# Two-layer macaron transformer block on one core: the last summed weight block of each down projection used at the very end, one gate/up chunk of the first layer by seven products instead of two, second quarter of x turned after the first products

## The chip, the cores and the metric

One core of a Trainium2 chip runs the whole program. The engines have their own in-order instruction streams: TensorE (PE in the profile; its weight loads are PEld), VectorE (DVE), ScalarE (ACT), GpSimd (POOL) and SyncE (SP), which here only issues DMAs. The metric is the device time of one execution in microseconds, median of several.

## The reference, cut to what matters

```python
D_MODEL = 1024; SEQ = 256; DEPTH = 2; D_FF = 2816

def swiglu(x, w_gate, w_up, w_down):
    return (jax.nn.silu(x @ w_gate) * (x @ w_up)) @ w_down

for l in range(DEPTH):
    x = x + 0.5 * swiglu(rms_norm(x, ffa_norm[l]), ffa_w_gate[l], ffa_w_up[l], ffa_w_down[l])
    x = x + hybrid_mixer(rms_norm(x, mix_norm[l]), ...)
    x = x + 0.5 * swiglu(rms_norm(x, ffb_norm[l]), ffb_w_gate[l], ffb_w_up[l], ffb_w_down[l])
return rms_norm(x, final_norm)
```

All arrays are float32. The change touches only the four feed-forward stages (swiglu), which are called A0, B0, A1 and B1 below, after their weights (ffa, ffb) and layer. The mixers (attention and its projections) stand between A and B of a layer.

## The kernel before, in words

**Three matmuls for one product.** float32 operands are split into a high part in fp32r (a rounded copy, `whi` or `xhi`) and the rest (`wlo`, `xlo`). A product is high by high, low by high, high by low: lines 323, 324 and 325, three matmuls of 128x512. A weight block of 1 MB is loaded into a `raw` buffer (five of them), and split in two halves of 128x1024: ACT copies the half to `whi` (line 304), then DVE subtracts to get `wlo` (line 283). There are six pairs of `whi`/`wlo` buffers, so splits run at most three blocks ahead of PE.

**Seven products for eight.** The 256 tokens are two halves t, the 1024 inputs two halves, and gate and up columns of a 512-wide chunk c are two blocks. Gate and up of a chunk are thus a 2x2 by 2x2 block product. It is done directly (in a plan: `g2` and `u2`, 48 matmuls each with both token halves), or as Strassen-Winograd by seven products of 12 matmuls (`11 51 21 31 61 71 41` for chunk 1, the first digit being the product). Five of the seven use sums of blocks. Sums of x are made by DVE (`fnhi`, `fohi` hold their two parts). Sums of weights are made by the DMA queue of POOL: the `raw` buffer of the block before is kept, and once both its halves are split, a DMA with `accum_op=OP.add` adds the next block into it. Products 1, 5, 6, 4 form one such chain in one `raw` buffer, 3 and 7 another, 2 stands alone. A chain keeps its buffer from its first to its last product.

**The down projection.** The same seven products (`1d` to `7d`) do rows 0 to 511 and 1024 to 1535 of the 2816 rows of w_down against chunks 0 and 2 of the hidden values; the other rows are done directly, in blocks of 256 rows (`p2`, `p8`, ..., 24 matmuls each: two token halves by two column halves). The list `DOWN` is the order. Its last `TAIL = 2` blocks, p7 and p10, are done column half by column half and token half by token half, so that each of the four output blocks (t, c) is closed (`close`, line 846: DVE adds it to x) as early as its last product, and the next stage's norm can turn it (four transposes on PE, line 409, then `xhi` on ACT and `xlo` on DVE).

**Order of the work.** A planner (class `Flow`) steps generators by estimated times and writes each engine's stream in that order. Splits are written in the order of the plan's blocks (`units_`), `raw` loads on SP's queue likewise, sums on POOL's queue. `ARRIVE` and `ARRIVE_X` are the planner's times at which the first blocks of weights and the quarters of x arrive; until the planner's time 8, PE is fed warm-up matmuls (`warm`) whenever it has nothing else.

Of the kernel before, what the change touches and what calls it, by code (L numbers as in the profile page):

```python
# [30 lines left out]
TAIL = 2  # L31
# [7 lines left out]
COLD = 5.0  # L39
WARM = 8  # L40
ARRIVE = [4.4, 5.2, 6.7, 7.4], [8.9, 9.6, 11.1, 11.8]
ARRIVE_X = [3.5, 5.9, 8.1, 10.3]
HOP = 0.3
PLANS = ("g0 u0 g2 11 u2 51 21 31 13 61 71 g4 41 53 23 33 u4 63 73 h5 43".split(),) + (
    "g0 u0 11 g2 51 21 31 u2 61 71 13 g4 41 53 23 33 u4 63 73 h5 43".split(),) * 3
DOWN = "1d p2 2d p8 5d p9 3d p3 6d p6 7d 4d p7 p10".split()
AHEAD = 1
AC = 0.1
DV = 0.06
# [85 lines left out]
def hybrid_kernel(ctx, tc, x_in, ffa_norm, ffa_w_gate, ffa_w_up, ffa_w_down, mix_norm, w_in,  # L135
# [14 lines left out]
    fl = Flow()  # L150
# [5 lines left out]
    def bank(tag, bufs):  # L156
        return psum.tile([128, 512], F32, name=tag, tag=tag, bufs=bufs)
# [63 lines left out]
    def order(src, a, b, loads=1, **k):  # L221
        return Unit(Raw(src, a, b, loads), fine=loads > 1, **k)
# [92 lines left out]
    def free_w(u=None):  # L315
        fl.put("w", 0)

    def cols(w, c0, n, kh):
        return w[kh * 512:(kh + 1) * 512, c0:c0 + n].rearrange("(k p) n -> p k n", p=128)
# [8 lines left out]
    def prod(ps, xs, t, k, u, i, sl, first, last):  # L328

        xh, xl = (z[:, k, t * 128:(t + 1) * 128] for z in xs)  # L330
        wh, wl = (z[:, sl] for z in u.part(i))
        prod3(ps, xh, xl, wh, wl, first, last)
# [113 lines left out]
    def ffn_units(wg, wu, wd, plan, first):  # L446

        us = {}  # L450
        chain = {}

        def block(c, m, kh):
            if c == "d":
                r = (0, 2)[kh] * 512
                return wd[r:r + 512, m * 512:(m + 1) * 512].rearrange("(k p) n -> p k n", p=128)
            return cols((wg, wu)[m], c * 512, 512, kh)

        def step(key, c, p, m, kh, end):

            src = block(c, m, kh)
            if key not in chain:
                chain[key] = (Raw(src, 4, 512), None)
                r = chain[key][0]
            else:
                r = Sum(chain[key][0], src, chain[key][1])
            us[p, c] = Unit(r, done=end)
            chain[key] = (chain[key][0], us[p, c])

        for z in plan + DOWN:  # L470
            kind = z[0]
            c = "d" if z[1] == "d" else int(z[1:])
            if kind == "p":
                src = wd[c * 256:(c + 1) * 256].rearrange("(i p) n -> p i n", i=2)
                us["d", c] = order(src, 2, 1024)
            elif kind in "gu":
                m = "gu".index(kind)
                for kh in range(2):
                    us[z, kh] = order(block(c, m, kh), 4, 512, loads=4 if first and z == plan[0] else 1)
            elif kind == "h":  # L480
                for kh in range(2):
                    us[z, kh] = order([cols(wg, 2560, 256, kh), cols(wu, 2560, 256, kh)], 4, 512)
            elif kind in "1564":
                step(("x", c), c, kind, *{"1": (0, 0), "5": (1, 0), "6": (1, 1), "4": (0, 1)}[kind], kind == "4")
            elif kind in "37":
                step(("y", c), c, kind, *{"3": (1, 1), "7": (1, 0)}[kind], z == [q for q in plan + DOWN if q[0] in "37" and q[1:] == z[1:]][-1])
            else:
                step(("z", c), c, kind, 0, 1, True)
        return us

    def ffn(us, nm, nxt, plan, last=False):
# [6 lines left out]
        inner = [i for i, z in enumerate(plan) if z[0] in "1234567"]  # L498
# [96 lines left out]
        def plain(z, tag, first):  # L595
            c, then = int(z[1:]), {"g": gate, "u": up, "h": both}[z[0]]
            ps = {}
            for kh in range(2):
                u = us[z, kh]
                order_ = [(t, i) for t in range(T) for i in range(4)] if first and nm.gi else [(t, i) for i in range(4) for t in range(T)]  # L600
                for t, i in order_:
                    k = kh * 4 + i
                    yield nm.turned[k, t]
                    yield u.when(i)
                    if k == 0:
                        yield fl.get(tag)
                        ps[t] = bank(tag, 4 if tag == "acc" else 2)
                    prod(ps[t], nm.xs, t, k, u, i, slice(0, 512), k == 0, k == KT - 1)
                    if k == KT - 1:
                        fl.spawn(then(c, t, ps[t], tag))  # L610
                    yield
                    if t and i % 2:
                        free_w()
# [86 lines left out]
            fl.spawn(sums(), 1)  # L700


        dforms, dk = {}, {}

        def sums_d():
# [39 lines left out]
        for i, z in enumerate(plan):  # L745
            if i == len(plan) - AHEAD:
                fl.spawn(sums_d(), 1)
            if z[0] in "1234567":
                yield from product(z[0], int(z[1:]))
            else:  # L750
                yield from plain(z, "sb" if inner and i > inner[0] else "acc", i == 0)
        if last:
            yield from last()
        pd = {}
# [22 lines left out]
        def add_x(src, f, t, c):  # L777
            xv = x[:, t, c * 512:(c + 1) * 512]
            nc.vector.scalar_tensor_tensor(xv, src, f, xv, op0=OP.mult, op1=OP.add)
            e = fl.dve(512)  # L780
            event("x", t, c).set(e)
            return e

        def rest_d():
            yield event("D1")
            yield fl.get("p")
            s = md([128, 512], "p", NP)
            nc.scalar.activation(s, dk["1"], AF.Copy)
            e = fl.act(512)
            yield e  # L790
            fl.put("sb", 0, e)
            add_x(s, 0.5, 0, 0)
            yield event("D5")
            yield fl.get("p")
            w = md([128, 512], "p", NP)
            nc.scalar.activation(w, dk["5"], AF.Copy)
            fl.put("sb", 0, fl.act(512))
            yield event("D6")
            nc.vector.tensor_tensor(s, s, dk["6"], OP.subtract)
            e = fl.dve(512)  # L800
            fl.put("sb", 0, e)
            yield e
            nc.vector.tensor_tensor(w, w, s, OP.add)
            yield fl.dve(512)
            add_x(w, -0.5, 0, 1)
            yield event("D7")
            nc.vector.tensor_tensor(w, w, dk["7"], OP.add)
            yield fl.dve(512)
            nc.vector.tensor_tensor(s, s, dk["7"], OP.add)
            e = fl.dve(512)  # L810
            fl.put("sb", 0, e)
            yield e
            fl.put("p", 0, add_x(w, -0.5, 1, 1))
            fl.put("p", 0, add_x(s, 0.5, 1, 0))

        def product_d(p):
            u = us[p, "d"]
            alone = {"2": (0, 0), "3": (0, 1), "4": (1, 0)}.get(p)
            if p in "124":
                c, t = {"1": (0, 0), "2": (2, 0), "4": (2, 1)}[p]  # L820
                yield ev[c, t]
                left = [z[:, 4 * c:4 * c + 4, t * 128:(t + 1) * 128] for z in hs]
            else:
                yield event("dform", p)
                left = dforms[p]
            if alone:
                new = yield from bank_d(*alone)
                ps = pd[alone]
            for i in range(4):
                yield u.when(i)  # L830
                if i == 0 and not alone:
                    yield fl.get("sb")
                    ps, new = bank("sb", 2), True
                    dk[p] = ps
                wh, wl = u.part(i)
                prod3(ps, left[0][:, i], left[1][:, i], wh, wl, new and i == 0, i == 3)
                yield
                if i % 2:
                    free_w()
            event("D" + p).set(fl.clock + HOP)  # L840

        def close(t, c):
# [8 lines left out]
            nxt(t, c)  # L851

        fl.spawn(rest_d())
        for z in DOWN[:-TAIL]:
            if z[0] == "p":
                for t in range(T):
                    yield from down(int(z[1:]), t, (0, 1), t == 1)
            else:
                yield from product_d(z[0])
# [1 line left out]
        if not last:  # L861
            ends = [(t, c) for c, t in ends]
        for i, (t, c) in enumerate(ends):
            for z in DOWN[-TAIL:]:
                yield from down(int(z[1:]), t, (c,), i == 3)
            fl.spawn(close(t, c))

# [773 lines left out]
    units = []  # L1641
    plans = iter(PLANS)
    for i, (kind, _, w) in enumerate(layers):
# [10 lines left out]
    def start_x(q):  # L1654
        yield ARRIVE_X[q]
        yield from norms[0].turn((2 * q, 2 * q + 1), range(T))
# [122 lines left out]
```

## Time and profile before

| | |
|---|---|
| time, median of 3 runs | 997.96 us (996.79 to 998.6) |
| the profiled execution | 997.24 us, of which the profile's span is 995.5 us |
| PE, PEld busy | 98%, 82% |
| DVE, ACT, POOL busy | 81%, 65%, 7% |
| granted TensorE clock | 0.999 |
| DMA | 220.22 MB, 221 GB/s on average |

The profiled execution lies 0.72 us below the median of the runs. Matmuls overlap in the profile: one of 128x512 is shown as 0.39 us long, but the next starts 0.23 us after it. An idle time in brackets is counted from the shown end.

### The profile page before, as it was taken

To read this page: it belongs to the slowest core of one execution; us is meant where nothing else is said; L and a number is where in the kernel's file an instruction comes from. 1 tells how busy PE (TensorE), PEld (TensorE's weight loads), DVE (VectorE), ACT (ScalarE), POOL (GpSimd) and SP (SyncE) were. 2 spreads that over 40 slices of the span, in tenths; PEclk is the share of its full clock that TensorE was granted. 3 is DMA by queue.
4 is the path that set the end of the run, shared out by engine and by line. 5 is a ranking of instruction groups with operands and counts; after the bars stand their busy time and mean duration, and the time that the engine had idled before them with its cause. 6 is when DMAs were issued, how large, how long until landed. Compare 5 with 4: busy or idle time off the path is not lost.

```text
span 995.5 us, 14306 instructions
## 1 busy us (share of the span) xinstructions
PE 979.6 (98%) x5220; PEld 817.1 (82%) x5220; DVE 807.6 (81%) x1469; ACT 647.2 (65%) x1109; POOL 74.3 (7%) x77
## 2 busy tenths in 40 slices
PE   9999999999999999999999999999999999999997
PEld 8877888798987888888788888878988878888885
DVE  6889795898787978798688778868878789688966
ACT  7566564658785666666467565655687766666654
POOL 1021011100000011101001110101000001110110
PEclk9999999999999999999999999999999999999999
DMA  9899979463743699989859999894745337999891
GB/s 336 268 198 302 292 216 281 150 211 101 282 130 125 175 249 298 258 252 244 262 168 232 287 273 256 232 258 125 250 146 201 120 114 225 266 281 276 255 211 43
DMA packets 111415, 220.22 MB, mean 221 GB/s; under 512 B 3976, under 2 KB 23568, under 8 KB 111344
## 3 DMA queue, kind: packets, MB, share of 16 engines
q1 hardware_dynamic: 85056, 167.46, 47.8%
q0 software_dynamic: 25984, 51.32, 29.1%
q8 instruction: 41, 0.67, 0.3%
q10 hardware_dynamic: 304, 0.53, 0.1%
q14 instruction: 30, 0.25, 0.1%
HBM read 218.24 MB, written 1.05 MB: 220 GB/s over the span
## 4 chain that ended last, share of the span: by engine, by line
PE 81%; DMA 8%; DVE 6%; issue 3%; ACT 1%; POOL 0%; POOLq 0%; ACTq 0%; DVEq 0%
PE acc L324 14%; PE acc L323 14%; PE acc L325 14%; PE sb L324 7%; PE sb L325 7%; PE sb L323 7%; DMA raw<-in_ffa_w_down_dram 4%; DVE wlo L283 4%; DMA raw<-in_ffa_w_up_dram 3%; PE acc L340 2%; PE acc L341 2%; PE acc L342 2%; PE acc L1206 2%; PE tb L1186 2%; PE tb L555 2%
## 5 line engine op out<-in xcount | busy, mean ns | idle before, releaser
L283 DVE TENSOR_TENSOR wlo<-raw,whi 128x1024 fp32r<-128x1024 f32 (+2 forms) x428 | 478.4, 1139 | 112.7 <-ACT whi L304 112.2
L304 ACT ACTIVATE whi<-raw 128x1024 fp32r<-128x1024 f32 (+2 forms) x428 | 412.1, 993 | 191.1 <-PE sb L325 44.5
L323 PE MATMUL acc<-whi,xhi 128*128 128x512 f32 (+1 forms) x336 | 131.3, 391 | 0.0
L324 PE MATMUL acc<-wlo,xhi 128*128 128x512 f32 (+1 forms) x336 | 128.0, 381 | 0.0
L325 PE MATMUL acc<-whi,xlo 128*128 128x512 f32 (+1 forms) x336 | 127.8, 380 | 0.0
L323 PE MATMUL sb<-whi,xhi 128*128 128x512 f32 x304 | 119.3, 392 | 0.0
L324 PE MATMUL sb<-wlo,xhi 128*128 128x512 f32 x304 | 118.4, 390 | 0.8 <-DVE wlo L283 0.8
L325 PE MATMUL sb<-whi,xlo 128*128 128x512 f32 x304 | 118.5, 390 | 0.0
L324 PE MATMUL acc<-wlo,hhi 128*128 128x512 f32 x256 | 100.3, 392 | 3.0 <-DVE wlo L283 3.0
L323 PE MATMUL acc<-whi,hhi 128*128 128x512 f32 x256 | 100.9, 394 | 0.0
L325 PE MATMUL acc<-whi,hlo 128*128 128x512 f32 x256 | 99.9, 390 | 0.0
L325 PEld LDWEIGHTS acc<-whi,xlo 128*128 128x128 f32 x336 | 63.1, 188 | 12.2
L323 PEld LDWEIGHTS acc<-whi,xhi 128*128 128x128 f32 x336 | 63.3, 189 | 11.5 <-issue 0.7
L324 PEld LDWEIGHTS acc<-wlo,xhi 128*128 128x128 f32 x336 | 63.2, 188 | 10.7
L324 PEld LDWEIGHTS sb<-wlo,xhi 128*128 128x128 f32 x304 | 57.1, 188 | 12.9 <-DVE wlo L283 1.2
L325 PEld LDWEIGHTS sb<-whi,xlo 128*128 128x128 f32 x304 | 57.1, 188 | 12.0
L323 PEld LDWEIGHTS sb<-whi,xhi 128*128 128x128 f32 x304 | 57.1, 188 | 11.6
L324 PEld LDWEIGHTS acc<-wlo,hhi 128*128 128x128 f32 x256 | 48.1, 188 | 14.7 <-DVE wlo L283 5.2
L340 PE MATMUL acc<-xhi,whi 128*128 128x256 f32 x192 | 56.7, 295 | 0.0
L325 PEld LDWEIGHTS acc<-whi,hlo 128*128 128x128 f32 x256 | 48.1, 188 | 9.9
L323 PEld LDWEIGHTS acc<-whi,hhi 128*128 128x128 f32 x256 | 48.1, 188 | 9.7
L342 PE MATMUL acc<-xhi,wlo 128*128 128x256 f32 x192 | 54.2, 282 | 0.0
(266 smaller groups left out, 1659.0 us busy)
## 6 DMA issues: line engine op xcount, KB each, us to landing
raw<-in_ffa_w_down_dram SPq DMA_DIRECT2D x20, 1024.0 KB, 7.6
raw<-in_w_in_dram SPq DMA_DIRECT2D x20, 1024.0 KB, 6.1
raw<-in_ffb_w_gate_dram SPq DMA_DIRECT2D x20, 1024.0 KB, 5.6
raw<-in_ffb_w_down_dram SPq DMA_DIRECT2D x20, 1024.0 KB, 7.3
raw<-in_ffa_w_gate_dram SPq DMA_DIRECT2D x18, 1024.0 KB, 8.6
raw<-in_ffa_w_up_dram SPq DMA_DIRECT2D x16, 1024.0 KB, 6.8
raw<-in_ffb_w_up_dram SPq DMA_DIRECT2D x16, 1024.0 KB, 5.7
raw<-in_ffa_w_up_dram POOLq DMA_DIRECT2D x12, 1024.0 KB, 9.7
```

The source lines that it names most:

```text
L283: nc.vector.tensor_tensor(view(u, lo, i, True), source(u, i), view(u, hi.bitcast(F32), i, True), OP.subtract)
L304: nc.scalar.activation(view(u, u.halves[-1][0], i, True), source(u, i), AF.Copy)
L323: nc.tensor.matmul(ps, xh, wh, start=first, stop=False, skip_group_check=True)
L324: nc.tensor.matmul(ps, xh, wl, start=False, stop=False, skip_group_check=True)
L325: nc.tensor.matmul(ps, xl, wh, start=False, stop=last, skip_group_check=True)
L340: nc.tensor.matmul(ps, wh, xs[0][:, k], start=first and j == 0, stop=False, skip_group_check=True)
L341: nc.tensor.matmul(ps, wh, xs[1][:, k], start=False, stop=False, skip_group_check=True)
L342: nc.tensor.matmul(ps, wl, xs[0][:, k], start=False, stop=last, skip_group_check=True)
L555: nc.tensor.transpose(ps[:, j * 128:(j + 1) * 128], h[:, j * 128:(j + 1) * 128], ident)
L1186: nc.tensor.transpose(ps[:, j * 128:(j + 1) * 128], pp[:, i * n + s_ * 128:i * n + (s_ + 1) * 128], ident)
L1206: nc.tensor.matmul(grp.o[u * 64:(u + 1) * 64, h // 2 * 128:(h // 2 + 1) * 128], val(s_), pT[:, j * 128:(j + 1) * 128], start=u not in grp. ...
```

## The change

Three things change. The list `DOWN` puts `4d`, the last product of the chain 1, 5, 6, 4, behind p7 and p10. `4d` works on one output block only, (1, 1), which is closed last; so p7 and p10 of the other three blocks go before it, and it stands ahead of p7 and p10 of (1, 1). For that the two column halves of w_down swap roles in the seven products (`1 - m`, and the flipped indices in `add_x` and `alone`). In the first stage's plan chunk 3 is done directly (`g3`, `u3`) and chunk 1 alone by seven products, in another order. And the planner is told that the second quarter of x arrives at 7.0 (was 5.9) and the third at 8.6 (was 8.1). The condition on `"sb"` only says which PSUM banks the direct products behind the last of the seven use.

```diff
-ARRIVE_X = [3.5, 5.9, 8.1, 10.3]
+ARRIVE_X = [3.5, 7.0, 8.6, 10.3]
-PLANS = ("g0 u0 g2 11 u2 51 21 31 13 61 71 g4 41 53 23 33 u4 63 73 h5 43".split(),) + (
+PLANS = ("g0 u0 g2 u2 11 g4 51 21 31 u4 61 71 g3 41 u3 h5".split(),) + (
     "g0 u0 11 g2 51 21 31 u2 61 71 13 g4 41 53 23 33 u4 63 73 h5 43".split(),) * 3
-DOWN = "1d p2 2d p8 5d p9 3d p3 6d p6 7d 4d p7 p10".split()
+DOWN = "1d p2 2d p8 5d p9 3d p3 6d p6 7d p7 p10 4d".split()
...
-                return wd[r:r + 512, m * 512:(m + 1) * 512].rearrange("(k p) n -> p k n", p=128)
+                return wd[r:r + 512, (1 - m) * 512:(2 - m) * 512].rearrange("(k p) n -> p k n", p=128)
...
-                yield from plain(z, "sb" if inner and i > inner[0] else "acc", i == 0)
+                yield from plain(z, "sb" if inner and inner[0] < i < inner[-1] else "acc", i == 0)
...
-            add_x(s, 0.5, 0, 0)
+            add_x(s, 0.5, 0, 1)
...
-            alone = {"2": (0, 0), "3": (0, 1), "4": (1, 0)}.get(p)
+            alone = {"2": (0, 1), "3": (0, 0), "4": (1, 1)}.get(p)
...
-        for z in DOWN[:-TAIL]:
+        for z in DOWN[:-TAIL - 1]:
...
         for i, (t, c) in enumerate(ends):
-            for z in DOWN[-TAIL:]:
+            if i == 3:
+                yield from product_d("4")
+            for z in DOWN[-TAIL - 1:-1]:
                 yield from down(int(z[1:]), t, (c,), i == 3)
             fl.spawn(close(t, c))
```

How the instructions move is seen at two places. The first is the start of PE's stream: line 1728 (1731 after the change) is the warm-up, line 409 a turn of a quarter of x by four transposes, lines 323 to 325 the first products. Before:

```order
L1728 MATMUL acc<-ident,ones 128x128 x5
L1677 MATMUL tb<-ident,g_89 128x8
L409 MATMUL tb<-ident,x 128x128 x4
L1728 MATMUL acc<-ident,ones 128x128 x5
L409 MATMUL tb<-ident,x 128x128 x4
L1728 MATMUL acc<-ident,ones 128x128
L323 MATMUL acc<-whi,xhi 128x512
L324 MATMUL acc<-wlo,xhi 128x512
L325 MATMUL acc<-whi,xlo 128x512
```

and with the change:

```order
L1731 MATMUL acc<-ident,ones 128x128 x5
L1680 MATMUL tb<-ident,g_89 128x8
L409 MATMUL tb<-ident,x 128x128 x4
L1731 MATMUL acc<-ident,ones 128x128 x8
L323 MATMUL acc<-whi,xhi 128x512
L324 MATMUL acc<-wlo,xhi 128x512
L325 MATMUL acc<-whi,xlo 128x512
L409 MATMUL tb<-ident,x 128x128 x4
```

The second quarter's turn moves from ahead of the first three matmuls to behind them, and thirteen warm-ups stand where eleven were.

The second place is DVE's stream at the end of the first down projection. The `wlo` rows are splits. Before, `raw_988` is the block of 4d, `raw_1377` that of p7, `raw_1426` that of p10 and `raw_1481` the next stage's first; line 846 closes an output block:

```order
L283 TENSOR_TENSOR wlo_1515<-raw_988,whi_1514 128x1024
L779 SCALAR_TENSOR_TENSOR x_78<-p_1400,x_78 128x512
L283 TENSOR_TENSOR wlo_1528<-raw_988,whi_1527 128x1024
L283 TENSOR_TENSOR wlo_1545<-raw_1377,whi_1544 128x1024
L283 TENSOR_TENSOR wlo_1558<-raw_1377,whi_1557 128x1024
L807 TENSOR_TENSOR p_1400<-p_1400,sb_1547 128x512
L283 TENSOR_TENSOR wlo_1568<-raw_1426,whi_1567 128x1024
L809 TENSOR_TENSOR p_1254<-p_1254,sb_1547 128x512
L283 TENSOR_TENSOR wlo_1579<-raw_1426,whi_1578 128x1024
L779 SCALAR_TENSOR_TENSOR x_78<-p_1400,x_78 128x512
L779 SCALAR_TENSOR_TENSOR x_78<-p_1254,x_78 128x512
L283 TENSOR_TENSOR wlo_1592<-raw_1481,whi_1591 128x1024
```

With the change p10's block is `raw_1405`, 4d's `raw_975`, the next stage's first `raw_1460`, and closing is line 847 (p7's two splits stand just ahead of these rows):

```order
L283 TENSOR_TENSOR wlo_1526<-raw_1405,whi_1525 128x1024
L283 TENSOR_TENSOR wlo_1537<-raw_1405,whi_1536 128x1024
L808 TENSOR_TENSOR p_1379<-p_1379,sb_1528 128x512
L283 TENSOR_TENSOR wlo_1547<-raw_975,whi_1546 128x1024
L810 TENSOR_TENSOR p_1253<-p_1253,sb_1528 128x512
L283 TENSOR_TENSOR wlo_1558<-raw_975,whi_1557 128x1024
```

and, six rows further on, behind the closing of the first two blocks and their turned copies:

```order
L847 SCALAR_TENSOR_TENSOR x_78<-acc_1268,x_78 128x512
L283 TENSOR_TENSOR wlo_1643<-raw_1460,whi_1642 128x1024
L418 SCALAR_TENSOR_TENSOR xlo_1591<-tb_1648,gall_79,xhi_1590 128x128 x4
L283 TENSOR_TENSOR wlo_1668<-raw_1460,whi_1667 128x1024
L847 SCALAR_TENSOR_TENSOR x_78<-acc_1287,x_78 128x512
```

4d's splits move from ahead of p7's to behind p10's, and the next stage's first two splits from ahead of the first closed block to around the last turn.

## Rows read from the trace of the kernel before

**Rows 1.** The page: busy time of the engines, share of the span, instructions.
```profile
PE 979.6 (98%) x5220; PEld 817.1 (82%) x5220; DVE 807.6 (81%) x1469; ACT 647.2 (65%) x1109; POOL 74.3 (7%) x77
```

**Rows 2.** Waits of PE by releaser: us in total, times, longest.
```profile
PE acc L324 <- DVE wlo L283: 6.3, 8, 1.1
```

**Rows 3.** PE in order of time, ends of down stages A0, B0, A1: start, length.
```profile
177.99 0.39 PE L323 MATMUL acc<-whi,hhi 128*128 128x512 f32 x1
...
180.71 0.39 PE L323 MATMUL acc<-whi,hhi 128*128 128x512 f32 x1
...
181.43 0.40 PE L323 MATMUL acc<-whi,hhi 128*128 128x512 f32 x1
182.59 0.50 PE L324 MATMUL acc<-wlo,hhi 128*128 128x512 f32 x1 [0.76 <-DVE wlo L283]
182.93 0.40 PE L325 MATMUL acc<-whi,hlo 128*128 128x512 f32 x1
...
491.70 0.50 PE L324 MATMUL acc<-wlo,hhi 128*128 128x512 f32 x1 [0.77 <-DVE wlo L283]
...
670.44 0.50 PE L324 MATMUL acc<-wlo,hhi 128*128 128x512 f32 x1 [0.66 <-DVE wlo L283]
...
672.17 0.50 PE L324 MATMUL acc<-wlo,hhi 128*128 128x512 f32 x1 [0.77 <-DVE wlo L283]
```

**Rows 4.** The chain that ended last: start, length, what; stage A0.
```profile
68.00 5.39 DMA raw<-in_ffa_w_up_dram
73.90 1.22 DVE wlo L283
...
160.86 11.78 DMA raw<-in_ffa_w_down_dram
172.74 1.07 ACT whi L304
```

**Rows 5.** ACT in order of time, end of A0's down stage.
```profile
165.40 2.01 ACT L304 ACTIVATE whi<-raw 128x1024 fp32r<-128x1024 f32 x2 [3.83 <-DMA raw<-in_ffa_w_down_dram]
172.74 7.87 ACT L304 ACTIVATE whi<-raw 128x1024 fp32r<-128x1024 f32 x8 [5.33 <-DMA raw<-in_ffa_w_down_dram]
186.56 1.14 ACT L415 ACTIVATE xhi<-tb,gall 128x128 fp32r<-128x128 f32 x4 [5.95 <-PE tb L409]
187.58 0.65 ACT L431 ACTIVATE junk<-x 128x512 f32<-128x512 f32 x1
```

**Rows 6.** DVE in order of time, the same stretch.
```profile
173.84 1.23 DVE L283 TENSOR_TENSOR wlo<-raw,whi 128x1024 fp32r<-128x1024 f32 x1 [3.66 <-ACT whi L304]
...
185.40 1.21 DVE L283 TENSOR_TENSOR wlo<-raw,whi 128x1024 fp32r<-128x1024 f32 x1
187.74 1.13 DVE L418 SCALAR_TENSOR_TENSOR xlo<-tb,gall,xhi 128x128 fp32r<-128x128 f32 x4 [1.13 <-ACT xhi L415]
188.78 1.28 DVE L846 SCALAR_TENSOR_TENSOR x<-acc,x 128x512 f32<-128x512 f32 x2
```

**Rows 7.** PE in order of time, stage A0's gate and up.
```profile
58.16 0.66 PE L555 MATMUL tb<-ident,sg 128*128 128x128 f32 x4 [0.31 <-DVE sg L580]
...
72.39 0.50 PE L324 MATMUL acc<-wlo,fohi 128*128 128x512 f32 x1 [0.62 <-DVE wlo L283]
...
75.17 0.50 PE L324 MATMUL acc<-wlo,fohi 128*128 128x512 f32 x1 [1.13 <-DVE wlo L283]
...
77.63 0.50 PE L324 MATMUL sb<-wlo,xhi 128*128 128x512 f32 x1 [0.80 <-DVE wlo L283]
```

**Rows 8.** PE in order of time, the start.
```profile
4.90 2.32 PE L1728 MATMUL acc<-ident,ones 128*128 128x128 f32 x10
7.04 0.62 PE L409 MATMUL tb<-ident,x 128*128 128x128 f32 x4
7.50 0.39 PE L1728 MATMUL acc<-ident,ones 128*128 128x128 f32 x2
7.64 0.48 PE L323 MATMUL acc<-whi,xhi 128*128 128x512 f32 x1
```

More of the change, by code (lines that the diff above doesn't have):

```diff
@@ L804, in rest_d @@
             yield fl.dve(512)
-            add_x(w, -0.5, 0, 1)
+            add_x(w, -0.5, 0, 0)
             yield event("D7")
@@ L812, in rest_d @@
             yield e
-            fl.put("p", 0, add_x(w, -0.5, 1, 1))
-            fl.put("p", 0, add_x(s, 0.5, 1, 0))
+            fl.put("p", 0, add_x(w, -0.5, 1, 0))
+            fl.put("p", 0, add_x(s, 0.5, 1, 1))
         def product_d(p):
             u = us[p, "d"]
-            alone = {"2": (0, 0), "3": (0, 1), "4": (1, 0)}.get(p)
+            alone = {"2": (0, 1), "3": (0, 0), "4": (1, 1)}.get(p)
             if p in "124":
```

## The prediction

> **What bounds the kernel now.** The page comes first: PE is busy for 979.6 of 995.5 us [rows 1]. Its clock is 0.999 for the whole span, so what can be won is matmuls that are left out and waits of PE. The view of waits by releaser gives 6.3 us of PE's idle time, in eight waits, to splits on DVE [rows 2]. PE's order of time says where they are. Four lie at the ends of down projections, one each in A0 and B0 and two in A1, and two in A0's gate and up, where a third split (on `sb`) and a gated value are waited for too [rows 3, 7]. The other two, some 1.6 us, lie at the ends of the mixers and aren't touched. B1's end has none.
>
> What a wait costs is more than its bracket. Twelve matmuls from 177.99 to 180.71 [rows 3] make 0.227 us from start to start. Ahead of the first, the matmul at 181.43 is followed at 182.59, after 1.16 us, where without a wait the next starts after 0.23: lost 0.93, that is the bracket of 0.76 and 0.16 of overlap. The matmul behind the wait is followed after 0.34 and not 0.23, so 0.11 more. A wait costs bracket + 0.27.
>
> Why the ends wait is in the chain. The sum for 4d is issued at 160.86 and lands 11.78 us later; only then does ACT split it, at 172.74 [rows 4]. ACT's row shows what stands behind: it idled for 5.33 us, and then ran eight splits in one go, 4d's two, p7's, p10's and the next stage's first block's [rows 5]. DVE idled 3.66 us before the same point and then had no pause up to the 185.40 row [rows 6]. PE caught up with it at p10's second half.
>
> **The change part by part.** *The down ends.* 4d's splits go behind p7's and p10's, whose loads are plain. The matmul at 181.43 is the tenth of p7 and p10 for the first block [rows 3], so that block began 9 x 0.227 earlier, at 179.4, and 4d with its 12 matmuls at 176.7. With the change p7 and p10 of three blocks, 36 matmuls or 8.2 us, begin at 176.7, and 4d at 184.9. The sum that lands at 172.64 is then 12 us early and not 4. p7's splits can use the time in which ACT and DVE idled. p10's need the two pairs that p6 holds until 7d begins, 12 matmuls ahead of p7, at 174.0. From there, with 0.2 for the last matmul to finish, `whi` takes 1.07 and the two `wlo` 1.23 each: 177.7, and p10's second half is first used by the eleventh matmul, at 179.0. The cover is 1.3 us. I take all four waits as gone: brackets 0.76 + 0.77 + 0.66 + 0.77 = 2.96, and 4 x 0.27 = 1.08, together **-4.04 us**. B1 has nothing to lose.
>
> *What is late next.* The next stage's first block can't be split before 4d gives back its pairs. In the last block's 24 matmuls 4d's 12 come first, six to a half. Behind its first half there are 18 matmuls and a turn (4.1 + 0.46 = 4.5 us) until the next stage's first product; the split takes 1.07 + 1.23, so it is in time. The second half is given back 2.7 us ahead, and is used six matmuls (1.4 us) into the next stage. On ACT it stands behind the turned copies (1.14) and the squares (0.65 and a short read) [rows 5], so it goes in order: release of the first half 4.3 us ahead of the next stage, split 1.07, copies 1.14, squares 0.85, split 1.07 ends 0.2 us ahead; DVE's 1.22 on top gives 1.0 us behind the start, needed at 1.4 + 0.23. Cover 0.5 us. DVE then closes the last block (0.6 of the 1.28 for two [rows 6]), for which the turn of it waits at 2.0: cover 0.3. If this cover is gone, a split's 1.2 us at each of three ends is the price, 3.6 in all. I put 0.25 us in for it, between 0 and 3.6, near the bottom, since each step is a row of the same kind.
>
> *The first stage's plan.* Chunk 3 takes 96 matmuls directly where it took 84: 12 x 0.227 = **+2.72 us**. Three plain loads and four sums become four plain loads, and three blocks' splits go, six halves each on ACT and DVE. The waits come from sums that have too little time: in the chain a sum ends (5.39 us from 68.00), then DVE's split at 73.90, then PE's wait at 75.17 [rows 4, 7]. Between a product and the next of its chain there are 36 matmuls before 61 and 24 before 71 now, 8.2 and 5.4 us, in which the sum and two halves' splits must fit but for the lead that splits have on PE. With the change there are 72 and 60, 16.3 and 13.6 us; before 51 and 41 it stays at 48 and 60. Against a sum of up to 11.78 and 2.3 us for a first half, 13.6 and a lead of one block (2.7) leave 2.2 of cover. I take the four waits as gone: brackets 0.31 + 0.62 + 1.13 + 0.80 = 2.86, overlap 4 x 0.16 = 0.64, and 0.11 behind each of the three that stood inside products: **-3.83 us**. The least is no gain, if other waits come; the most is this.
>
> *The start.* The quarter's turn costs what it cost, 7.04 to 7.50; behind it stood one warm-up in two passes, 7.50 to 7.64 [rows 8]. The change has two warm-ups, four passes, more, and the first product doesn't come earlier for the turn: 7.04 + six passes, then product, then turn. A pass takes 0.07 (7.50 to 7.64, two) to 0.214 (4.90 to 7.04, ten); the four transposes, one pass each at the faster pace, took 0.115. So 4 x 0.115 = **+0.46 us**, between 0.28 and 0.86. PE has no wait between 7.64 and 20 now, so nothing gives this back. With the change the turned quarter is needed three products and a turn later, 3 x 0.68 + 0.46 = 2.5 us; copies of as many columns take 1.14 on ACT and 1.13 on DVE, one behind the other [rows 5, 6]: cover 0.2, and half as long a copy (one of the quarter's two) is all that the first use needs.
>
> *The other edits* cost nothing: the flipped column halves swap which block is read and where it is added, with the same instructions; and p2, which asks for the PSUM banks of u3 and h5, stands 12 matmuls (1d, 2.7 us) behind h5, in which they are emptied; without that cover it would be one gated half's 0.6 us or so.
>
> **Sum.** -4.04 + 0.25 - 3.83 + 2.72 + 0.46 = -4.44 us. 997.24 - 4.44 = **992.8 us** for an execution like the profiled one; by the median shown, 0.7 higher, which the range holds.
>
> **The rivals.**
>
> *New waits in the first stage.* If a sum is still late, at 51, where the time between products stays at 48 matmuls (10.9 us), or DVE is the limit there, which is what the wait at 58.16 for a gated value speaks for, 3.83 us are lost in another place. Against it: 51 doesn't wait now at the same distance, DVE has six splits fewer, and POOL's queue four DMAs. Then -4.04 + 0.25 + 2.72 + 0.46 = -0.6: 996.6.
>
> *Half the down waits stay.* p10's splits still wait for p6's pairs, at 174.0, 1.3 us later than ACT begins now. For it: DVE's splits and sums behind that are as many as now. Against: 4d's two, with a third of the work, are no longer ahead of p10's. -4.44 + 2.02 = -2.4: 994.8.
>
> *Not the sum's landing.* The late splits at the ends could be held by the six pairs alone, and the sum could have landed long before; then moving 4d changes nothing there, and -3.83 + 2.72 + 0.46 = -0.65 is left: 996.6. Against it is the chain, in which ACT's split at 172.74 follows the landing directly. The Trainium skill, "DMA: Bandwidth & Descriptors", section "Anatomy of one DMA — SWDGE (gpsimd) path", gives a fit of 2.0 us and bytes over 436e3 per us for one DMA of POOL's queue, 4.4 us for 1 MB, by which the sum would land at 165.3 and this rival would hold. The trace has 11.78 us for it, and decides.
>
> *Slower.* The next stage's first block is split too late. If both its halves come only behind the last closed block, PE waits 1.07 + 1.23 + 1.14 = 3.4 us at each of three ends, 10.3 in all: 992.6 + 10.3 = 1002.9. It decides from (4.69 + 2) / 3 = 2.2 us an end on. For it: the pairs are all held, 4d's two, p7's and p10's, where now 4d's are free 13 us earlier. Against: the 18 matmuls of cover above.
>
> **How the numbers follow.** A run of this kernel tells apart about 0.2%, 2 us. Chances: all as summed 0.72; half the down waits stay 0.12; new waits in the first stage 0.08; not the landing 0.03; slower 0.05. The first two are faster: 0.84; the next two lie within 0.2%: 0.11; slower 0.05. The range goes down to 991.2 (the start at its lower bound and nothing lost at the next stages give -4.87 and 992.4, and the lowest run shown is 1.2 below the median) and up to 995.6 (half the down waits stay, 994.8, and 0.7 for the median); above it lie the last three cases, 0.16.
>
> **What would show it.** Right: no wait of PE for a split at the ends of A0, B0 and A1, ACT's split of 4d late in a row that starts earlier, and in A0's gate and up no wait over 0.5 us; PE's first product near 7.64 and the second turn at about 8.4. Wrong: a wait of PE on the first `wlo` of the next stage, or on the turn of the last closed block; a wait in A0 at 51 or 41; 4d waiting for its sum after all, near 185.

## The result, and the profile after

The changed kernel takes 992.31 us in the median of eight runs (991.28 to 995.48), the kernel before 997.94 beside it (996.59 to 999.89): a ratio of 0.9949, interval 0.9937 to 0.9962. Run again on another chip (e12, below) it was 0.9931, 0.9915 to 0.9946. The forecast was 992.8, 991.2 to 995.6, faster. The profiled execution took 991.77 us, its span is 990.0, 5.5 less than before. First the page: the busy row that answers to [rows 1], the shares by engine of the chain that ended last, and the software DMA queue (packets, MB, share):

```profile
PE 980.0 (99%) x5236; PEld 820.0 (83%) x5236; DVE 799.9 (81%) x1458; ACT 643.4 (65%) x1101; POOL 68.9 (7%) x73
...
PE 98%; DVE 1%; ACT 1%; issue 0%; POOL 0%; POOLq 0%
...
q0 software_dynamic: 23872, 47.12, 27.0%
```

The last two of these rows in the kernel before:

```profile
PE 81%; DMA 8%; DVE 6%; issue 3%; ACT 1%; POOL 0%; POOLq 0%; ACTq 0%; DVEq 0%
...
q0 software_dynamic: 25984, 51.32, 29.1%
```

PE does 16 matmuls more (12 of the plan, four passes of warm-ups) and yet ends earlier. The last chain holds no DMA any more, where DMAs had 8% of it: 98% of it is PE's own work. The view of PE's waits by releaser has one row for splits, and that of its weight loads (PEld) one that is new:

```profile
PE acc L324 <- DVE wlo L283: 1.6, 2, 0.8
```
```profile
PEld tb L409 <- DVE x L847: 1.4, 3, 0.5
```

Eight waits of 6.3 us [rows 2] are two of 1.6, and these two stand at the ends of the mixers, which the change doesn't touch. The three of PEld are a turn's: that of the third of the four output blocks, at the ends of A0, B0 and A1.

ACT in order of time at the end of A0, in answer to [rows 5]:

```profile
164.41 2.14 ACT L304 ACTIVATE whi<-raw 128x1024 fp32r<-128x1024 f32 x2
166.84 1.06 ACT L304 ACTIVATE whi<-raw 128x1024 fp32r<-128x1024 f32 x1 [0.29 <-PE sb L325]
171.60 3.10 ACT L304 ACTIVATE whi<-raw 128x1024 fp32r<-128x1024 f32 x3 [3.70 <-PE acc L325]
175.00 1.06 ACT L304 ACTIVATE whi<-raw 128x1024 fp32r<-128x1024 f32 x1 [0.29 <-PE sb L325]
181.56 1.14 ACT L415 ACTIVATE xhi<-tb,gall 128x128 fp32r<-128x128 f32 x4 [5.50 <-PE tb L409]
...
185.49 1.06 ACT L304 ACTIVATE whi<-raw 128x1024 fp32r<-128x1024 f32 x1 [0.54 <-ACT junk L431]
...
188.48 2.02 ACT L304 ACTIVATE whi<-raw 128x1024 fp32r<-128x1024 f32 x2
```

Before, eight splits went in one go at 172.74 behind 5.33 us of waiting for a DMA. Now no split waits for a DMA: p7's go ahead, p10's two and 4d's two (the rows at 171.60 and 175.00) wait for PE, which gives pairs back, and the next stage's first block is split at 185.49 and 188.48, around its copies. 4d's sum is issued at 159.0 and lands 10.3 us later, at 169.3; the last of 4d's splits on DVE (at 177.34, 1.22 us long) ends some five us ahead of its first matmul. The new turn wait, on DVE and PE:

```profile
184.38 1.13 DVE L418 SCALAR_TENSOR_TENSOR xlo<-tb,gall,xhi 128x128 fp32r<-128x128 f32 x4 [0.52 <-ACT xhi L415]
185.42 0.68 DVE L847 SCALAR_TENSOR_TENSOR x<-acc,x 128x512 f32<-128x512 f32 x1
```
```profile
185.70 0.39 PE L325 MATMUL acc<-whi,hlo 128*128 128x512 f32 x1
186.16 0.65 PE L409 MATMUL tb<-ident,x 128*128 128x128 f32 x4
```

The third block is closed at 185.42, behind four copies, and its turn begins at 186.16, 0.46 behind the matmul ahead of it where 0.23 is the pace: 0.23 lost. The same turns at 494.15 and 672.97 cost 0.21 and 0.20. (Of the next stage's first two splits, which the section on the change puts around the last turn, it is thus the third block's turn that stands between them.) The last closed block waits for nothing: DVE closes it at 190.72, in the next stage, and its turn at 192.13 follows the matmul ahead of it, at 191.89, at the usual pace.

From the first product of one phase to that of the next, the 5.47 us that the span is shorter lie as follows (the start: up to the turn of x's third quarter; a stretch that spans an end runs from the down projection's first product to the next down projection's):

| stretch | before | after | difference | forecast |
|---|---|---|---|---|
| start | 9.80 | 9.81 | +0.01 | +0.46 |
| A0's gate and up from there | 122.52 | 120.96 | -1.56 | -1.11 |
| A0's down to B0's | 308.93 | 307.71 | -1.22 | |
| B0's down to A1's | 179.75 | 178.81 | -0.94 | -3.79 in three |
| A1's down to B1's | 309.71 | 308.01 | -1.70 | |
| B1's down to the end | 64.76 | 64.70 | -0.06 | 0 |

### The profile page after: what moved, and what is told of

Same layout as the page of the kernel before. It is cut to its first block, busy times and chain, and to the rows that moved or that the text cites. A ratio compares the mean times of both kernels' runs of the same rounds, so it can differ in the third digit from the quotient of the medians.

```text
span 990.0 us, 14315 instructions
## 1 busy us (share of the span) xinstructions
PE 980.0 (99%) x5236; PEld 820.0 (83%) x5236; DVE 799.9 (81%) x1458; ACT 643.4 (65%) x1101; POOL 68.9 (7%) x73
## 4 chain that ended last, share of the span: by engine, by line
PE 98%; DVE 1%; ACT 1%; issue 0%; POOL 0%; POOLq 0%
PE acc L323 18%; PE acc L324 18%; PE acc L325 18%; PE sb L325 8%; PE sb L323 8%; PE sb L324 8%; PE acc L340 2%; PE acc L341 2%; PE acc L342 2%; PE tb L555 2%; PE acc L1209 2%; PE tb L1189 2%; PE tb L409 1%; PE acc L1378 1%; PE sb L1315 1%; PE sb L1258 1%
## 5 line engine op out<-in xcount | busy, mean ns | idle before, releaser
L283 DVE TENSOR_TENSOR wlo<-raw,whi 128x1024 fp32r<-128x1024 f32 (+2 forms) x422 | 472.2, 1139 | 116.3 <-ACT whi L304 115.7
L323 PE MATMUL acc<-whi,xhi 128*128 128x512 f32 (+1 forms) x372 | 145.8, 392 | 0.0
L324 PE MATMUL acc<-wlo,xhi 128*128 128x512 f32 (+1 forms) x372 | 142.0, 382 | 0.0
L325 PE MATMUL acc<-whi,xlo 128*128 128x512 f32 (+1 forms) x372 | 141.9, 381 | 0.0
L323 PE MATMUL sb<-whi,xhi 128*128 128x512 f32 x288 | 113.1, 393 | 0.0
L325 PE MATMUL sb<-whi,xlo 128*128 128x512 f32 x288 | 112.2, 390 | 0.0
L324 PE MATMUL sb<-wlo,xhi 128*128 128x512 f32 x288 | 112.1, 389 | 0.0
L325 PEld LDWEIGHTS acc<-whi,xlo 128*128 128x128 f32 x372 | 69.9, 188 | 13.5
L323 PEld LDWEIGHTS acc<-whi,xhi 128*128 128x128 f32 x372 | 70.1, 189 | 12.6 <-issue 0.7
L324 PEld LDWEIGHTS acc<-wlo,xhi 128*128 128x128 f32 x372 | 70.0, 188 | 11.9
L325 PEld LDWEIGHTS acc<-whi,hlo 128*128 128x128 f32 x256 | 48.1, 188 | 10.2
```

Source lines behind the costliest of these rows:

```text
L283: nc.vector.tensor_tensor(view(u, lo, i, True), source(u, i), view(u, hi.bitcast(F32), i, True), OP.subtract)
L323: nc.tensor.matmul(ps, xh, wh, start=first, stop=False, skip_group_check=True)
L324: nc.tensor.matmul(ps, xh, wl, start=False, stop=False, skip_group_check=True)
L325: nc.tensor.matmul(ps, xl, wh, start=False, stop=last, skip_group_check=True)
```

## Experiments

The theory is the forecast's: 4d's sum lands late and holds the splits queued behind 4d's on ACT and DVE; in A0's gate and up, sums with too little distance between a chain's products make the waits. The rivals: the pairs alone hold the splits; the distance of a chain is not what matters, DVE's load is. Medians are set against the kernel before on the same chip. Lost time is from start to start of two matmuls, less the usual 0.23.

**e1, the down projections alone** (against the changed kernel):

```diff
-ARRIVE_X = [3.5, 7.0, 8.6, 10.3]
+ARRIVE_X = [3.5, 5.9, 8.1, 10.3]
-PLANS = ("g0 u0 g2 u2 11 g4 51 21 31 u4 61 71 g3 41 u3 h5".split(),) + (
+PLANS = ("g0 u0 g2 11 u2 51 21 31 13 61 71 g4 41 53 23 33 u4 63 73 h5 43".split(),) + (
```

> The change at the end of the down projections alone; the first stage's plan and the arrival table of x are those of before. Theory (the landing of 4d's sum holds the late splits): the four waits at the ends of A0, B0 and A1 are gone, 3.8 to 4.0 us less than before, about 994.0 for 997.9 (0.996); A0's gate and up keep their four waits. Rival (the six pairs alone hold the splits; what the changed kernel won comes from the first stage): no more than 1 us less than before.

994.47 for 998.25, ratio 0.9966 (0.9953 to 0.9978): 3.8 less. The down ends are free of waits for a split (the third block's turn loses 0.21 at each, as in the changed kernel), and A0's gate and up keeps its own: PE's waits of 0.8 to 1.3 us of lost time at 59.0, 73.3, 76.1 and 78.5.

**e2, the first stage's plan alone** (against the kernel before):

```diff
-PLANS = ("g0 u0 g2 11 u2 51 21 31 13 61 71 g4 41 53 23 33 u4 63 73 h5 43".split(),) + (
+PLANS = ("g0 u0 g2 u2 11 g4 51 21 31 u4 61 71 g3 41 u3 h5".split(),) + (
```

> The first stage's plan alone (one chunk by seven products instead of two, 12 more matmuls); the down projections and the arrival table are those of before. Theory (the sums had too little time, and each wait costs more than its bracket): 3.8 to 4.2 us of waits go and 2.7 come in as matmuls, so 1.1 to 1.5 us less than before, about 996.6 (0.9985 to 0.999); the four waits at the down ends stay. Rival (a wait costs its bracket alone, 2.86): the same time as before within 0.3 us.

996.07 for 998.25, ratio 0.9977 (0.9967 to 0.9986): 2.2 less, more than the theory gave. A0's gate and up are 1.54 shorter, as in the changed kernel. The rest is in a place where it wasn't expected: A0's down end has no wait any more, with the order of before. 4d's sum lands there 39.0 us behind the down projection's first product and not 40.3. ACT's row:

```profile
170.42 4.85 ACT L304 ACTIVATE whi<-raw 128x1024 fp32r<-128x1024 f32 x5 [4.40 <-DMA raw<-in_ffa_w_down_dram]
```

ACT still waits for the landing, but 2.3 us earlier, and PE no longer catches up. This is the plan's doing and no accident of one execution: in the six profiled executions with this plan the sum lands at 38.6 to 39.2 in A0, and in the seven with two chunks by seven products that have a sum there at 40.3 to 44.4. B0's and A1's ends wait as before, so e1's and e2's gains overlap at one end.

That allows a graded test, later landing against more time lost: twelve ends in four kernels with the order of before (the kernel before, e2, and e3 and e8 below). Landing is that of 4d's sum behind the down projection's first product, lost is by how much the matmuls that wait start late, both worked out from the traces:

| landing, us | 38.97 | 40.03 | 40.32 | 40.50 | 40.85 | 40.95 | 40.96 | 41.13 | 41.22 | 41.62 | 42.09 | 44.44 |
|---|---|---|---|---|---|---|---|---|---|---|---|---|
| lost, us | 0 | 0.69 | 0.93 | 0.94 | 1.39 | 1.49 | 1.49 | 1.67 | 1.75 | 1.87 | 2.11 | 4.15 |
| kernel, end | e2 A0 | e3 A1 | before A0 | before B0 | e3 B0 | e8 B0 | e8 A1 | e3 A0 | before A1 | e2 B0 | e2 A1 | e8 A0 |

The later the landing, the more is lost, without an exception. (At e8's A0 4d itself waits, too.) The row leaves out the 0.11 us behind each wait, and losses too short for a bracket; with them the three ends of the kernel before lose 1.04, 1.26 and 1.97, 4.27 in all. In the changed kernel the sums land at 38.55, 40.80 and 41.26 and nothing waits for them.

**e5, 4d's block loaded plainly** (against the kernel before; 4d's weights then lack the three blocks that were added before):

```diff
+            elif z == "4d":
+                step(("w", c), c, kind, 0, 1, True)
...
-                step(("x", c), c, kind, *{"1": (0, 0), "5": (1, 0), "6": (1, 1), "4": (0, 1)}[kind], kind == "4")
+                step(("x", c), c, kind, *{"1": (0, 0), "5": (1, 0), "6": (1, 1), "4": (0, 1)}[kind], kind == "4" or z == "6d")
```

> The kernel before, with the block of weights for 4d loaded plainly into a buffer of its own and not added to three others (the product 4d then lacks those three blocks of the down weights, and the chain of sums ends at 6d; products, splits and their order are as before). Theory (the landing holds the splits): the four waits at the down ends go, about 4 us less than before, 994. Rival (the six pairs alone hold them): the waits stay, 997.9.

993.67 for 998.42, ratio 0.9954 (0.9941 to 0.9966): 4.8 less. No wait is left at the three ends, with the order, the pairs and the splits of before. The three stretches are 1.17, 1.28 and 1.94 shorter, 4.39 in all, close to the 1.04, 1.26 and 1.97 that their ends had lost. In A0 4d's block now lands 36.7 us behind the down projection's first product. The pairs alone hold nothing; it is the sum's landing. The edit also gives 4d's block another buffer and takes a DMA off POOL's queue, so one could ask whether p7's or p10's load was what came late. It wasn't: in A0 of the kernel before these land at 157.57 and 165.74, and are split behind 4d's, from some 174.7 on.

**e3 and e4, the arrival table alone**, put into the kernel before and taken out of the changed one:

```diff
-ARRIVE_X = [3.5, 5.9, 8.1, 10.3]
+ARRIVE_X = [3.5, 7.0, 8.6, 10.3]
```

> The arrival table of x alone: the turn of x's second quarter goes behind two warm-ups and the first product. Theory (four more warm-up passes ahead of the first product, at 0.07 to 0.21 us each): the second product begins 0.3 to 0.9 us later at an equal clock, the time 0.4 us longer than before, 998.3. Rival (the start was free in the changed kernel, where the second product came 0.08 us earlier): the same time as before within 0.1 us, whenever the clock rises.

> The changed kernel with the arrival table of before. Theory (the later turn costs four warm-up passes): 0.4 us less than the changed kernel, about 991.9 for 992.3. Rival (the later turn is free, or spares a wait for x's second quarter): the changed kernel's time, 992.3, or up to 0.5 more.

e3: 998.83 for 998.25, ratio 1.0010 (0.9999 to 1.0022). e4: 993.98 for 998.25, ratio 0.9959 (0.9947 to 0.9971), which overlaps the changed kernel's first ratio and lies just above its second. e3's interval holds both of its theories, and e4's 0.4 us less is not borne out. The times don't tell more; the traces do. PE at the start, changed kernel:

```profile
4.91 2.55 PE L1731 MATMUL acc<-ident,ones 128*128 128x128 f32 x16
7.21 0.47 PE L323 MATMUL acc<-whi,xhi 128*128 128x512 f32 x1
...
7.98 0.60 PE L409 MATMUL tb<-ident,x 128*128 128x128 f32 x4
8.34 0.48 PE L323 MATMUL acc<-whi,xhi 128*128 128x512 f32 x1
```

and e4:

```profile
4.90 1.71 PE L1731 MATMUL acc<-ident,ones 128*128 128x128 f32 x10
7.24 0.63 PE L409 MATMUL tb<-ident,x 128*128 128x128 f32 x4 [0.63 <-DMA x<-in_x_dram]
7.71 0.39 PE L1731 MATMUL acc<-ident,ones 128*128 128x128 f32 x2
7.85 0.48 PE L323 MATMUL acc<-whi,xhi 128*128 128x512 f32 x1
```

With the old table PE stands and waits for x's second quarter; with the new one it does warm-ups and the first product in that time. Over the profiled executions the turn of the third quarter begins at 9.80, 10.00, 10.01, 10.28, 10.35 and 10.38 with the old table (mean 10.14), and at 9.42 to 10.46 in eight with the new one (mean 9.96). Five of the six with the old table wait for the quarter, 0.3 to 1.1 us of lost time; only the profiled one of the kernel before, where the quarter had landed as PE came to it at 7.04, didn't. The turned quarter costs nothing on the average. e4's profile loses more far from the start, 0.9 us at 556.4 for a gated value (see e11).

**e6, 4d a block earlier** (against the changed kernel):

```diff
-            if i == 3:
+            if i == 2:
                 yield from product_d("4")
```

> The changed kernel with 4d ahead of the third block of p7 and p10 and not of the fourth, so that it begins 24 matmuls (5.4 us) and not 36 (8.2) behind 7d, and gives its pairs back 12 matmuls earlier. Theory (the sum lands 4 us behind the old place of 4d, so 5.4 us are enough; what is left at the turn of the last closed block, some 0.2 us an end, is the next stage's first block split late): the same time as the changed kernel or up to 0.6 us less, 991.7 to 992.3. Rival (the sum needs more than 5.4 us where it lands latest): a wait for 4d's split at one or more ends, 1 us or more each, 993.3 or above.

991.46 for 998.42, ratio 0.9931 (0.9919 to 0.9944). The time is as the theory had it, though it can't be told from the changed kernel's (0.9949 and 0.9931). In the trace the turns no longer wait, nothing waits for 4d, and the three stretches are 0.50 shorter than the changed kernel's. The reason isn't the one in the text above. The third block's turn waited because DVE had the second block's copies to do ahead of closing it; now 4d's 12 matmuls stand ahead of the third block's, and that block is closed later, at 187.53, behind copies that end at 186.4.

**e11, two blocks earlier** (`if i == 1`):

> The changed kernel with 4d ahead of the second block of p7 and p10, 12 matmuls (2.7 us) behind 7d. Theory (before the change the waits at an end grew with the landing of 4d's sum, from none at 39.0 us behind the down projection's start to 2.1 at 42.1; 4d is now asked for at 47 us, and its splits of 2.3 behind p7's and p10's must fit): the same as with 4d ahead of the third block where the sum lands by 42 us, within 0.5 us of 991.5. Rival (4d's splits stand behind p7's and p10's eight, in about 5 us of ACT and DVE, too long for 2.7 us of matmuls): waits on 4d's split at the ends, 1 us or more each, 994 or above.

992.59 for 998.52, ratio 0.9936 (0.9921 to 0.9951). The ends are free of waits, so eight splits ahead of 4d's aren't too many. But 1.1 us over the theory; in its profile 1.5 us are lost in A1's gate and up, on a gated value. PE's row there, and ACT's:

```profile
556.14 1.10 PE L555 MATMUL tb<-ident,sg 128*128 128x128 f32 x6 [1.13 <-DVE sg L580]
```
```profile
550.83 3.92 ACT L304 ACTIVATE whi<-raw 128x1024 fp32r<-128x1024 f32 x4 [6.96 <-DMA raw<-in_ffa_w_up_dram]
```

A sum of the up weights and the plain gate load issued behind it (540.2) land late; that load takes 14.6 us here and 10.2 in the changed kernel. In e4, where the same wait is, it is 12.8. Whether the earlier 4d causes the late landings stays open; by time e11 (992.23 to 993.63) can't be told from the changed kernel on the same chip (991.45 to 993.76).

**e7, the other stages' plan in the first, too** (against the changed kernel):

```diff
-PLANS = ("g0 u0 g2 u2 11 g4 51 21 31 u4 61 71 g3 41 u3 h5".split(),) + (
+PLANS = ("g0 u0 11 g2 51 21 31 u2 61 71 13 g4 41 53 23 33 u4 63 73 h5 43".split(),) + (
```

> The changed kernel with the plan of the other three stages in the first too: two chunks by seven products as before the change, but with 48 matmuls or more between the products of a chain, and 12 matmuls fewer than the changed kernel. Theory (the distance of a chain's products sets the waits): 2.7 us less than the changed kernel less what new waits come at the start, where 11 is asked for two plain chunks earlier; 989.6 to 991. Rival (the start's loads and DVE's work on the sums of x and the mask tables can't follow two chains of seven): waits of 3 us or more, so at or above the changed kernel's 992.3.

991.90 for 998.42, ratio 0.9935 (0.9921 to 0.9949): between the two. A0's gate and up are 0.9 shorter than in the changed kernel. No split is late now, but a gated value and a `z` are, 1.9 us in all:

```profile
67.42 1.31 PE L555 MATMUL tb<-ident,sg 128*128 128x128 f32 x8 [0.23 <-DVE sg L580]
...
78.78 0.63 PE L555 MATMUL tb<-ident,z 128*128 128x128 f32 x4 [1.18 <-DVE z L650]
```

**e8, the mask tables later** (against the kernel before):

```diff
     def late():
-        yield 40.0
+        yield 95.0
```

> The kernel before, with the mask tables made on DVE from 95 us and not from 40 us on the planner's clock. Theory (sums of weights with too little distance make A0's waits): they stay, 997.9 within 0.5. Rival (DVE's load by the tables makes them): they go, 3 to 4 us less than before, 994 to 995.

1000.97 for 998.42, ratio 1.0025 (1.0016 to 1.0033): neither. Of 4.0 us lost at six places in A0's first 115 us, one place of 0.87 is left up to 83 us, so most of what I had put down to distance alone needed DVE's work on the tables as well: without it the sums are issued 1 us earlier and no table row stands ahead of the split. But the same work at 95 us and after makes new waits there, and A0's down projection 4 us longer:

```profile
110.79 0.66 PE L555 MATMUL tb<-ident,sg 128*128 128x128 f32 x4 [0.55 <-DVE sg L580]
121.88 0.63 PE L555 MATMUL tb<-ident,z 128*128 128x128 f32 x4 [0.43 <-DVE z L650]
176.44 0.50 PE L323 MATMUL acc<-whi,hhi 128*128 128x512 f32 x1 [0.85 <-ACT whi L304]
177.70 0.50 PE L324 MATMUL acc<-wlo,hhi 128*128 128x512 f32 x1 [0.76 <-DVE wlo L283]
183.44 0.50 PE L324 MATMUL acc<-wlo,hhi 128*128 128x512 f32 x1 [0.77 <-DVE wlo L283]
185.18 0.50 PE L324 MATMUL acc<-wlo,hhi 128*128 128x512 f32 x1 [0.77 <-DVE wlo L283]
```

**e9, e10 and e12, what goes together:** e9 is the changed kernel with e6's and e7's edits, e10 is e9 with `yield 145.0` in `late()`, e12 the changed kernel again, all on one chip.

> The changed kernel with both: 4d ahead of the third block of p7 and p10, and the other stages' plan in the first stage. Theory (the two act on waits in different places): 0.8 us less for the turns of the last closed blocks and some 0.4 less for the plan, 1.2 below the changed kernel on the same chip, about 991.0. Rival (with seven products of chunk 3 the sum for 4d lands later, 40.4 us behind the down projection's start and not 38.6, and 24 matmuls are too few for it in the first stage): a wait for 4d's split at the end of A0 and the changed kernel's time or more.

> As the run before, with the mask tables made from 145 us on the planner's clock and not from 40. Theory (with 48 matmuls between products, what is left of waits in A0's gate and up is DVE's work on the mask tables among the splits): the waits for gated values and for z near 67 and 78 us go, 1.9 us less than the run before, if A0's down end keeps free of new ones; 989. Rival (they come from the sums' landing, or DVE's work comes back as waits in A0's down projection, as the tables made from 95 us did): the same time as the run before, or more.

> The changed kernel as it is, on the same chip as the runs beside it, so that they can be set against it without the kernel before between. Theory (its executions differ by waits on landings alone): 992.3, within 0.6; at the start, without a wait for x's second quarter. Rival: a wait for that quarter in this execution too, where the clock rises early.

Against 998.52: e9 991.31, ratio 0.9921 (0.9906 to 0.9936); e10 991.82, 0.9922 (0.9904 to 0.9940); e12 992.02, 0.9931 (0.9915 to 0.9946). e9 has the lowest median of all, 0.7 below the changed kernel beside it, but their runs overlap (990.40 to 991.98 and 991.45 to 993.76), so the better version is likely, not settled. Its two waits in A0 are e7's, 2.4 us of lost time, and no end waits. e10's theory, 989, is missed, and its rival, the same time or more, came. In e10 the wait for `z` is gone and the one for a gated value stays:

```profile
66.80 0.66 PE L555 MATMUL tb<-ident,sg 128*128 128x128 f32 x4 [0.62 <-DVE sg L580]
```

A0's gate and up are 1.5 shorter than in e9, of which 0.4 comes back as a wait for a turn at 182.0; 2.0 more are lost at 863.6 in this execution, behind a sum that took 14.2 us. The tables are thus one part of what is left in A0, and not the wait for the gated value. e12 came as its theory had it: its start has no wait for x, and its first product is at 6.82.

## Why the prediction was right, by its steps

**The down ends** (-4.04, with +0.25 for what is late next) came as -3.86 in the three stretches. The cause was the one named: e5 takes the landing away, with the order, the pairs and the splits as they were, and gains 4.39 there, and the twelve ends show no exception. The rival of the pairs falls with it. The other, that half the waits stay because p10's splits wait for p6's pairs, falls with ACT's and DVE's rows: p10's last split on DVE ends at 175.1 (in a stage that begins 1.55 earlier), where the forecast had 177.7 and the need 179.0. The price of a wait, bracket and 0.27, holds for the four, 4.04. Two more losses at B0's end, 0.10 and 0.11 at 489.97 and 490.30, were too short for a bracket and not counted; with them it is 4.27, and e5 and e6, which have neither these waits nor that of a turn, gain 4.39 and 4.36. That -3.86 lies so near the forecast's -3.79 is in part luck: the waits gave 0.23 more than forecast, what is late next took 0.39 more, and 0.23 of the gain in the stretches lies outside their ends.

**What is late next** was sized too small and seen in the wrong place. The turn of the last closed block, for which the step had a cover of 0.3 us, came in time (192.13). The wait is at the turn of the block before it, the third: 0.23, 0.21 and 0.20, 0.64 and not 0.25. What the third block's closing stands behind on DVE isn't a split of the next stage but the four turned copies of the second block; the step didn't look at this block. The slower rival, 2.2 us an end, was far off.

**The first stage's plan** gave -1.56 for -1.11. The added matmuls cost what they should; the waits gave 4.28 for 3.83. Two more, of 0.23 ahead of 81.85 and 0.21 ahead of 113.39, stood in the trace of before below the view's brackets and went too. The reason given was half of it, and one reading behind it was wrong. The 5.39 us from 68.00 [rows 4] aren't a sum's time: the sum issued at 68.00 lands 13.84 us later, at 81.84. The chain, asked for this stretch alone, shows what the split at 73.90 stood behind (line 902 and the next ones make the mask tables, and the first row is POOL's, which the view names by its DMA):

```profile
68.00 5.39 DMA raw<-in_ffa_w_up_dram
73.39 0.02 issue
73.41 0.18 DVE p L902
...
73.82 0.03 DVE km L905
73.85 0.04 issue
73.90 1.22 DVE wlo L283
```

So the longest of these waits, at 75.17, came from DVE's work on the tables, which itself waited for POOL; only the one at 72.39 follows a landing, that of a sum at 69.91. e8 says the same: without the tables at this time three of the four waits go, with the distance as it was. The plan answers to both, with 14 to 16 us between products and six splits fewer. It also shifts 4d's landing in A0 by 1.3 us or more (e2), so the down part and the plan pay for one wait twice. The medians, 3.8 and 2.2 alone and 5.6 together, fit that but are too near to show it.

**The start** is, for its size, the term that came out furthest off: +0.46 forecast, +0.01 in the two profiled executions. The step reckoned added passes at a given pace, and the warm-ups' pace is the execution's own: up to 7.04 us PE's stream is the same in both kernels, but a pass takes 0.21 up to 7.04 before and up to 6.17 after, and 0.11 from there, and so the first product came at 7.21. In e3 and e7, which have the new table, the pace doubles at 6.9 and at 7.2, and the third quarter's turn begins at 10.18 and 10.34. For a doubling as late as in the execution before, that makes 10.26, an estimate, 0.46 behind 9.80: at an equal pace the term was right, and its +0.01 is chance. What the step lacked is that with the old table PE waits for x in most executions, a wait that the profiled one didn't have and that covers the added passes.

By medians the kernel gained 5.6 us, by the profiles 5.5, and the sum had 4.44. Of the 1.03 between the profiles and the sum, 0.45 each is the start's and the plan's, and 0.13 lies in the four down stretches. The start's part is chance.

## What to carry to other kernels

Where engines run in order, ask of a late transfer what stands behind its consumer, not only who waits for it: moving one product behind two whose loads are plain freed three ends, though that product itself was never late. Look at several executions before costing an edit by tenths: a wait on a transfer may be absent from the one that is profiled, and an edit that covers it then looks like a cost. Two edits that remove the same wait are paid for it once, so single parts of a change can gain more alone than their share of the whole.

## What the runs showed of the hardware

The time from issue to landing of the same 1 MB transfer isn't a constant. 4d's sum took 10.3 to 14.3 us in 39 cases (three ends in thirteen profiled executions), and one plain gate load of A1 8.8, 10.2, 12.8 and 14.6 in four. The Trainium skill, "DMA: Bandwidth & Descriptors", section "Anatomy of one DMA — SWDGE (gpsimd) path", has a fit for one DMA of 2.0 us plus bytes over 436e3 per us, which makes an estimate of 4.4 us for 1 MB. None of the 39 cases comes near it, with other loads in flight. These landings, and not PE's work, may be what spreads the runs of one kernel, which no run here shows directly: on one chip e6, where little waits for a landing, lies within 991.19 to 991.84, and the kernel before within 996.48 to 999.51.

The pace of identical warm-up passes doubled, from 0.21 us each to 0.11, at 5.3 us in one execution (e12) and at 7.5 in another (e9) with the same stream of instructions on PE up to there, and moved the first product from 6.82 to 7.85. The view's granted clock doesn't show it: it is 1.00 from 5.0 to 8.0 us in both.
